# An S5 layer and prompt heads, placed differently against a paged attention

## The chip, the cores and the metric

The kernel runs on one core of a Trainium2 chip. The metric is the device time of one execution in microseconds, given as the median of several runs. Engines are called by the profile's names: PE is TensorE (matmuls and transposes), DVE is VectorE, ACT is ScalarE, POOL is GpSimd, and SP is SyncE, which issues most of the DMA transfers, in program order, from one queue of instructions.

## What is computed

One step of a two-layer decoder, for a prompt of 512 tokens and eight samples of four tokens each (544 columns in all, in most matmuls two halves of 272). Everything is float32. Layer 0 has the even mixer, which the change touches; layer 1, the memory attentions and the MLPs follow.

```python
def even_mixer(hn, pos, h0_re, h0_im, attend, p):
    proj = hn @ p['w_in']
    c_q, c_kv, k_r, u = proj[..., :o1], proj[..., o1:o2], proj[..., o2:o3], proj[..., o3:]
    cq = rms_norm(c_q, p['cq_norm'])
    qf = rms_norm((cq @ p['w_uq']).reshape(b, L, MLA_HEADS, MLA_QK), p['q_gain'])
    q = jnp.concatenate([qf[..., :MLA_NOPE], rope(qf[..., MLA_NOPE:], pos)], axis=-1)
    ckv = rms_norm(c_kv, p['ckv_norm'])
    kr = rope(k_r[:, :, None, :], pos)[:, :, 0]
    o_att = attend(q, ckv, kr).reshape(b, L, MLA_HEADS * MLA_V)
    o_s5, hr, hi = s5_ssm(u, h0_re, h0_im, p)
    return jnp.concatenate([o_att, o_s5], axis=-1) @ p['w_out'], ckv, kr, hr, hi
```

`attend` is causal attention over the prompt (8 heads) for the prompt rows. For the samples it is attention over 16 pages of 128 cached latent rows each (8 samples, so 128 pages), plus the four new tokens. `s5_ssm` is a complex diagonal recurrence over 32 groups of 16 channels with 64 states each, followed by a GELU and a gate: `z * sigmoid(z @ w_glu + b_glu)`.

## The kernel before

`even_mixer` first transposes x into h (the residual, [128, 8, 544], kept in SBUF to the end), then projects: u (S5's input), cq, ckv, q, and kv. Every weight comes through `load_w`: an SP load (wraw), a split into a high and a low part on ACT (wH) and DVE (wL), and three matmuls per product. The tile framework's scheduler orders the engines' instructions by its own estimates, except on SP in `decode_attention`, where `manual_schedule` keeps the order of the code.

`s5_layer` is called between the u and the cq projection, and the scheduler mixes its work into all the projections that follow. It has four tiles (4 x 128 channels). Of each tile, `s5_tables_of` builds tables on DVE and POOL (s5tmp, s5W, s5T, s5w), `s5_gather` fetches U by 16 small DMAs, and `s5_tile` runs the recurrence: matmuls s5X, products on DVE and POOL (s5g), scans on DVE, Hp, and 160 matmuls s5Y. A GELU (zt, z) and a split (zH, zL) follow. `s5_out` is the gate (glu, 96 matmuls) after kv.

`decode_attention` runs over 64 steps: 8 samples with 8 pairs of pages. In a step each page has its latents transposed (ct), split (cH, cL), and multiplied (24 kp matmuls for a pair, kp has two PSUM buffers); ACT squares kp (sq), DVE reduces the square (L1156) and adds the scores (L1155), and POOL raises the sums to the power -0.5 (L1161, once in two steps). `load_pages(b + 1)` first reads 16 page numbers (`page_numbers`, one register load each on SP), then issues 16 rope loads (krn) and 16 latent loads (cnat). It is called at page 4 of sample b, after `batch_end(b - 1)`, which does the softmax and the values of the sample before. At page 14 of a sample one prompt head is emitted (`prompt_head`: pqk transposes, four rounds of scores S, maximum, exponential Pm, transposes pPT, and then po), with three at sample 5, from q_tok, k_tok and v_tok in SBUF. At the end `beside` projects the memory (mkv, 192 matmuls), whose weights are loaded during sample 7, and then comes the output projection (ps_wo, 384 matmuls).

Of the kernel before, what the change touches and what calls it, by code (L numbers as in the profile page):

```python
# [105 lines left out]
class K:  # L106
    def __init__(self, tc, a, o, ctx):
# [11 lines left out]
        self.h = self.cp.tile([128, KT, NT], F32, name="h")  # L119
# [198 lines left out]
    def even_mixer(self, gs, beside):  # L318
# [11 lines left out]
        self.uT = utile("uT", F32)  # L330
        rs.enter_context(self.gemm_pools("left"))
        IN = main("even_in")
        s5s, cqs = ExitStack(), ExitStack()
        SP = s5s.enter_context(self.pool("s5main", side="left"))
# [5 lines left out]
        L = xp.tile([128, KT, NT], F32R, name="xgL")  # L340
        xts = self.load_x([CQ.tile([128, 6, NT], F32, tag=f"cq{x}", bufs=1, name=f"x{x}") for x in "HL"])
# [10 lines left out]
        self.s5_params(SP)  # L352
# [44 lines left out]
        self.gemm(w, KT, 0, 6, (H, L), ev, "cq")  # L397

# [32 lines left out]
        Q = qs.enter_context(self.pool("qkv", side="right"))  # L431
# [33 lines left out]
        for ch in range(2):  # L465
            wq = self.load_wk(a["w_mla_uq"][0], 6, 384 * ch, 384, f"uq{ch}")
            hs = slice(4 * ch, 4 * ch + 4)
            for t in (4, 0, 1, 2, 3):
# [23 lines left out]
                nc.vector.tensor_tensor(out=q[:, :, NOPE:], in0=q[:, :, NOPE:], in1=tmp[:rows], op=ALU.add)  # L492
        self.sample_heads(qTs, q_s, self.qgain)
# [36 lines left out]
        s5t.close()  # L530
        cqs.close()
        pg = self.page_numbers(0)
        self.s5_out()
        self.oatt = utile("oatt", F32)
        s5s.close()
        rs.close()
        gs.close()
        with ExitStack() as ds:
            dp = ds.enter_context(self.pool("dec1", side="left"))
            dp2 = ds.enter_context(self.pool("dec2", bufs=2, side="left"))  # L540
            ap = qs.enter_context(self.pool("patt", bufs=2, side="right"))
# [17 lines left out]
    def prompt_head(self, h, p, q_tok, k_tok, v_tok):  # L559
# [3 lines left out]
        for dst, src, gain in ((qT, q_tok, self.qgain), (kT, k_tok, 1.0)):  # L563
            ps = self.att_ps("pqk")
            for t in range(4):
                self.transpose(ps[:QK, t * 128:(t + 1) * 128], src[:, t, h, :])
# [22 lines left out]
        for j in range(4):  # L589
            c = b if j in (0, 3) else 64 - b  # L590
            nc.tensor.matmul(po[c:c + 64, j * 128:], v_tok[:, j, h, :], PT[:, j, j * 128:], start=(j < 2), stop=(j > 1),
                             skip_group_check=True, tile_position=(0, c))
# [197 lines left out]
    def s5_tables_of(self, ft, p, E):  # L790
# [6 lines left out]
        R = {}  # L797
        tmp = lambda: p.tile([128, 512], F32, tag="s2k", bufs=4, name="s5tmp")
# [3 lines left out]
        for i, (x, y, op) in enumerate((("bbr", "bbi", B), ("bbi", "bbr", A))):  # L802
            t1, t2 = [tmp()[:, :256].rearrange("p (q j c) -> p q j c", q=4, j=4) for _ in range(2)]
# [1191 lines left out]
```

## Time and profile before

| | us |
|---|---|
| median of the runs (3) | 1976.15 |
| lowest and highest | 1973.0, 1979.17 |
| profiled execution, its own time | 1978.92 |
| its span | 1977.2 |
| first kp of sample 0 | 254.5 |
| first kp of sample 4 | 411.2 |
| start of the last kp | 573.2 |
| first matmul of the output projection | 600.7 |

The span is what the profile covers. A window is a stretch of the span, with the busy time of each engine in it. The busy time of PE counts each matmul from its start to its modelled end, and matmuls overlap, so that the price of a matmul in a row of equal ones is the distance of two starts. The chain that ended last follows the work back from the last instruction, at each step to what released it.

### The profile page before, as it was taken

What the parts mean: (1) busy time and instruction counts of PE and PEld (TensorE: products, weight loads), DVE (VectorE), ACT (ScalarE), POOL (GpSimd) and SP (SyncE); (2) the same over time, 40 slices, a digit from 0 to 9 for tenths busy, and PEclk for the clock granted to TensorE, in tenths of its full rate; (3) what the DMA queues carried; (4) which work ended last, traced back from release to release, by engine and by line L of the source; (5) the groups of instructions that cost most, each with busy time, mean ns of one, the idle gap of its engine ahead of it and who ended that gap; (6) DMA issues with size and microseconds to landing.
All of it is one profiled execution on the core that took longest, in us unless ns stands there. A gap on an engine that the chain in (4) does not pass through costs nothing.

```text
span 1977.2 us, 39933 instructions
## 1 busy us (share of the span) xinstructions
PE 1911.8 (97%) x16089; PEld 1803.5 (91%) x16089; DVE 1165.2 (59%) x2264; ACT 804.5 (41%) x1546; POOL 471.4 (24%) x375
## 2 busy tenths in 40 slices
PE   8888899999999999999999999999999999999998
PEld 7876688889889979999999999999999799999998
DVE  7776566666765557433333568898865663434344
ACT  4455454455564444322222334444443432313131
POOL 4555246655552205000000110111132130000000
PEclk9988999999999999999999999999999999999999
DMA  6221221222334453322322332323325233223222
GB/s 151 72 56 36 69 69 49 67 74 52 100 107 99 141 174 95 95 86 87 95 86 86 91 100 83 104 78 97 91 70 168 91 105 87 86 87 95 86 86 78
DMA packets 317162, 179.42 MB, mean 91 GB/s; under 512 B 52241, under 2 KB 305266, under 8 KB 316978
## 3 DMA queue, kind: packets, MB, share of 16 engines
q1 hardware_dynamic: 289154, 164.47, 28.8%
q10 hardware_dynamic: 26224, 8.06, 1.7%
q0 software_dynamic: 1600, 4.34, 0.8%
q8 instruction: 127, 2.08, 0.4%
q14 instruction: 57, 0.47, 0.1%
HBM read 165.90 MB, written 9.82 MB: 89 GB/s over the span
## 4 chain that ended last, share of the span: by engine, by line
PE 88%; DVE 4%; ACT 2%; issue 2%; SPq 2%; DMA 1%; POOL 1%; ACTq 0%; DVEq 0%; POOLq 0%
PE ps_dn L191 19%; PE ps_up L191 19%; PE kp L1151 9%; PE ps_wo L191 5%; PE ps_hq L191 3%; PE ps_hi L191 3%; PE ps_hf L191 3%; PE ps_hg L191 2%; PE ps_mq L191 2%; PE ps_wmo L191 2%; PE mkv L191 2%; PE ps_u L191 1%; SPq L1026 1%; PE ct L290 1%; PE q L191 1%
## 5 line engine op out<-in xcount | busy, mean ns | idle before, releaser
L191 PE MATMUL ps_dn<-hidH,wH_dn 128*128 128x272 f32 x1024 | 211.4, 287 | 0.0
L191 PE MATMUL ps_dn<-hidH,wL_dn 128*128 128x272 f32 x1024 | 211.2, 288 | 0.0
L191 PE MATMUL ps_up<-actH_f,wH_up 128*128 128x272 f32 x1024 | 211.2, 287 | 0.0
L191 PE MATMUL ps_dn<-hidL,wH_dn 128*128 128x272 f32 x1024 | 210.7, 287 | 0.0
L191 PE MATMUL ps_up<-actH_f,wL_up 128*128 128x272 f32 x1024 | 210.5, 288 | 0.0
L191 PE MATMUL ps_up<-actL_f,wH_up 128*128 128x272 f32 x1024 | 210.4, 287 | 0.0
L1161 POOL TENSOR_TENSOR ss<-ss,nhalf 128x32 f32<-128x32 f32 x32 | 173.7, 5429 | 96.1 <-DVE ss L1159 92.9
L1266 DVE TENSOR_TENSOR h<-ps_dn,h 128x544 f32<-128x544 f32 x64 | 46.4, 725 | 207.1 <-PE ps_dn L191 207.1
L191 PEld LDWEIGHTS ps_dn<-hidL,wH_dn 128*128 128x128 f32 x1024 | 160.2, 188 | 0.0
L191 PEld LDWEIGHTS ps_up<-actL_f,wH_up 128*128 128x128 f32 x1024 | 160.0, 188 | 0.0
L191 PEld LDWEIGHTS ps_dn<-hidH,wL_dn 128*128 128x128 f32 x1024 | 159.6, 189 | 0.1
L191 PEld LDWEIGHTS ps_dn<-hidH,wH_dn 128*128 128x128 f32 x1024 | 159.5, 188 | 0.0
L191 PEld LDWEIGHTS ps_up<-actH_f,wL_up 128*128 128x128 f32 x1024 | 159.4, 188 | 0.0
L191 PEld LDWEIGHTS ps_up<-actH_f,wH_up 128*128 128x128 f32 x1024 | 159.4, 188 | 0.0
L166 ACT ACTIVATE wH_dn<-wraw_dn 128x1024 fp32r<-128x1024 f32 x64 | 68.1, 1064 | 216.5 <-PE ps_dn L191 154.8
L166 ACT ACTIVATE wH_up<-wraw_up 128x1024 fp32r<-128x1024 f32 x64 | 68.1, 1063 | 195.0 <-PE ps_up L191 99.1
L167 DVE TENSOR_TENSOR wL_up<-wraw_up,wH_up 128x1024 fp32r<-128x1024 f32 x64 | 83.5, 1305 | 107.8 <-ACT wH_up L166 105.7
L167 DVE TENSOR_TENSOR wL_dn<-wraw_dn,wH_dn 128x1024 fp32r<-128x1024 f32 x64 | 78.3, 1224 | 67.5 <-ACT wH_dn L166 65.3
L1154 ACT ACTIVATE sq<-kp 128x512 f32<-128x512 f32 x128 | 76.5, 597 | 95.6 <-PE kp L1151 56.1
L254 POOL TENSOR_TENSOR acc_x<-acc_x,sq 128x544 f32<-128x544 f32 x7 | 10.8, 1540 | 349.6 <-issue 327.2
L1156 DVE TENSOR_REDUCE ss<-sq 128x8 f32<-128x512 f32 x128 | 86.8, 678 | 0.0
L166 ACT ACTIVATE hidH<-mu 128x544 fp32r<-128x544 f32 x64 | 42.2, 660 | 101.0 <-DVE mu L1577 101.0
(738 smaller groups left out, 5081.8 us busy)
## 6 DMA issues: line engine op xcount, KB each, us to landing
wraw_up<-in_w_mlp_up_dram SPq DMA_DIRECT2D x64, 512.0 KB, 4.1
wraw_dn<-in_w_mlp_down_dram SPq DMA_DIRECT2D x64, 512.0 KB, 3.7
cnat<-in_cache_mla_latent_dram SPq DMA_DIRECT2D x128, 128.0 KB, 2.2
mkc<-in_cache_mem_k_dram SPq DMA_DIRECT2D x16, 512.0 KB, 6.3
wraw_w_mem_k<-in_w_mem_k_dram SPq DMA_DIRECT2D x8, 512.0 KB, 4.7
wraw_w_mem_v<-in_w_mem_v_dram SPq DMA_DIRECT2D x8, 512.0 KB, 3.7
wraw_wo<-in_w_out_even_dram SPq DMA_DIRECT2D x8, 512.0 KB, 4.0
wraw_mq<-in_w_mem_q_dram SPq DMA_DIRECT2D x8, 512.0 KB, 3.6
```

The source lines that it names most:

```text
L166: i = nc.scalar.activation(H, x, AF.Copy)
L167: sub.tensor_tensor(out=L, in0=x, in1=H.bitcast(F32), op=ALU.subtract)
L191: nc.tensor.matmul(out, x, sl(y), start=first and n == 0, stop=last and n == 2)
L254: nc.gpsimd.tensor_tensor(out=acc, in0=acc, in1=sq, op=ALU.add)
L290: self.nc.tensor.transpose(out, in_, self.ident[:p, :p])
L1026: load = lambda x, t, src: nc.sync.dma_start(x, src[bass.ds(pg[t], 1), 0].rearrange("o t c -> (o t) c"))
L1151: mm = nc.tensor.matmul(ps[:, hf, :272], x[:, t % 2, kt], wb[hf][y][:, kt], start=(kt == 0 and n == 0), stop=(kt == 1 and n == 2))
L1154: nc.scalar.activation(sq, ps[:, :, :256], AF.Square)
L1156: V.tensor_reduce(out=ss[:, t, :], in_=sq.rearrange("p f (h d) -> p (f h) d", h=4), op=A, axis=AX.X)
L1161: G.tensor_tensor(out=sf, in0=sf, in1=self.nhalf, op=ALU.pow)
L1266: self.nc.vector.tensor_tensor(out=halves(self.h[:, i, :]), in0=ps, in1=halves(self.h[:, i, :]), op=ALU.add)
```

## The change

S5 and the gate are taken out of the prologue and become a generator, `mixer_steps`, that `decode_attention` draws from after the page scores of each step. `s5_layer` yields twelve times per tile and `s5_out` five times, each half a step; then comes the load of head 0 (one step) and the eight heads at four steps each, where `load(h + 1)` is issued ahead of head h. For this

- the residual h is stored to DRAM (hd) after the transposes, its SBUF tile is freed, and it is loaded again, in eight pieces, ahead of the output projection;
- q, k and v of the prompt are stored to DRAM (qd, kd, vd: twelve stores) as they are made, their SBUF tiles are freed, and each head loads its three parts into a pool of two buffers;
- S5's temporaries are 256 wide instead of 512 (five buffers), U, w, g and Hp get two buffers, and all PSUM of S5 and the gate is the attention's `at` (two buffers), which the heads use too;
- `s5_params` runs after the cq projection.

The core of the diff:

```diff
@@ even_mixer
+        self.h = hs.enter_context(self.pool("hx", side="right")).tile([128, KT, NT], F32, name="hx")
+        self.hd = self.ctx.enter_context(self.pool("hd", space=bass.MemoryType.DRAM)).tile([128, KT, NT], F32, name="hd")
...
-        self.s5_params(SP)
+        nc.sync.dma_start(self.hd, self.h)
+        hs.close()
...
-        s5t = ExitStack()
-        self.s5_layer(*(s5t.enter_context(self.pool(n, side="left")) for n in ("s5E", "s5tile")))
...
         self.gemm(w, KT, 0, 6, (H, L), ev, "cq")
+        self.s5_params(SP)
...
+                if t < 4:
+                    nc.sync.dma_start(qd[:, :, t, :], q)
...
+            if t < 4:
+                nc.sync.dma_start(kd[:, :, t, :], k_tok[:, t])
+                nc.sync.dma_start(vd[:, :, t, :], v_tok[:, t])
...
-        self.s5_out()
...
-            self.decode_attention(dp, dp2, pg, qTs, kTs, lambda h: self.prompt_head(h, ap, q_tok, k_tok, v_tok), qs,
-                                  beside)
+            self.decode_attention(dp, dp2, pg, qTs, kTs, self.mixer_steps(utile, qs, qd, kd, vd), qs, beside)
...
+    def mixer_steps(self, utile, qs, qd, kd, vd):
+        nc = self.nc
+        with self.pool("s5E", side="right") as pe, self.pool("s5tile", side="right") as p:
+            for _ in self.s5_layer(pe, p):
+                yield 0.5
+        with self.pool("s5glu", bufs=2, side="right") as self.wp:
+            for _ in self.s5_out(self.wp):
+                yield 0.5
+        self.oatt = utile("oatt", F32)
+        ap = qs.enter_context(self.pool("patt", bufs=2, side="right"))
+        def load(h):
+            ts = [ap.tile([128, 4, x.shape[3]], F32, name=n) for n, x in (("q_tok", qd), ("k_tok", kd), ("v_tok", vd))]
+            for t, x in zip(ts, (qd, kd, vd)):
+                nc.sync.dma_start(t, x[:, h])
+            return ts
+        ts = load(0)
+        yield 1
+        for h in range(HEADS):
+            nx = load(h + 1) if h + 1 < HEADS else None
+            self.prompt_head(h, ap, *ts)
+            ts = nx
+            yield 4
@@ s5_tables_of, s5_tile
-        tmp = lambda: p.tile([128, 512], F32, tag="s2k", bufs=4, name="s5tmp")
+        tmp = lambda: p.tile([128, 256], F32, tag="s1k", bufs=5, name="s5tmp")
...
-        ps = self.psA("s5T")
+        ps = self.att_ps("s5T")
@@ decode_attention
-                if t == NPG - 2:
-                    for h in range(b, b + 1 if b < 5 else HEADS if b == 5 else b):
-                        head(h)
+                while due <= n - AHEAD:
+                    due += next(more, len(steps))
@@ before the output projection
+                self.h = es.enter_context(self.pool("h", side="left")).tile([128, KT, NT], F32, name="h")
+                for k in range(KT):
+                    nc.sync.dma_start(self.h[:, k, :], self.hd[:, k, :])
```

How the order changes, at three places. The first is PE where sample 4 takes over from sample 3: krT and krS belong to the keys of sample 4. Before:

```order
1633 L1151 MATMUL kp<-wk11H,cL 128x272
1634 L290 MATMUL krT<-ident,krn_3209 128x128 x4
1635 L1151 MATMUL kp<-wk10H,cH 128x272
...
1654 L1151 MATMUL kp<-wk11H,cH 128x272
1655 L1115 MATMUL krS<-qr,krT 128x128 x4
1656 L1151 MATMUL kp<-wk10L,cH 128x272
```

And now, where rows 1537 to 1632 are the 96 matmuls of the gate:

```order
1536 L980 MATMUL s5Y<-s5U,s5T 32x136 x4
1537 L190 MATMUL glu_5070<-zH_2980,wH_glu_5066 128x272
...
1632 L190 MATMUL glu_5268<-zH_5055,wL_glu_5264 128x272
1633 L289 MATMUL s5f<-ident,s5finp 16x128
...
1638 L289 MATMUL krT<-ident,krn_2039 128x128 x3
1639 L1157 MATMUL krS<-qr,krT 128x128 x4
1640 L289 MATMUL ct<-ident,cnat_2040 128x128 x4
```

The keys of sample 4 stood between kp matmuls of sample 3; now they stand behind the gate, and no kp stands between the last S5 matmul and them.

The second place is PE in a prompt head. Before (head 7, its third and fourth round of scores):

```order
2449 L1151 MATMUL kp<-wk11H,cL 128x272
2450 L290 MATMUL pPT<-ident,Pm 128x128 x3
2451 L572 MATMUL S<-kT,qT 128x512
2452 L574 LDWEIGHTS identb
2453 L574 MATMUL S<-causalb,identb 128x128
2454 L1151 MATMUL kp<-wk10H,cH 128x272
```

And now (head 1, ahead of the first kp of sample 5):

```order
1883 L605 MATMUL S<-causalb,identb 128x128
1884 L289 MATMUL pPT<-ident,Pm 128x128 x3
1885 L603 MATMUL S<-kT,qT 128x512
1886 L605 LDWEIGHTS identb
1887 L605 MATMUL S<-causalb,identb 128x128
1888 L289 MATMUL krT<-ident,krn_2034 128x128 x3
1889 L289 MATMUL pPT<-ident,Pm 128x128 x4
1890 L289 MATMUL krT<-ident,krn_2034 128x128
1891 L622 MATMUL po<-PT,v_tok 64x512
```

The rounds of a head had 12 or 24 kp matmuls between them; of this head and of heads 3, 5 and 7 they follow one another.

The third place is SP ahead of the page numbers (TENSOR_LOAD pt) of sample 5, with what each instruction waits for. Before:

```order
568 L1026 DMA cnat_3210<-in_cache_mla_latent_dram 128x256 [waits DMAHW4_49,PE_49]
569 L1026 ISA
570 L1026 DMA cnat_3210<-in_cache_mla_latent_dram 128x256 [waits DMAHW5_49,PE_49]
571 L1000 TENSOR_LOAD pt
572 L1000 ISA x2
```

And now, where the wait on PE in row 604 is for the output matmuls of head 0:

```order
598 L1068 DMA cnat_2040<-in_cache_mla_latent_dram 128x256 [waits DMAHW2_49]
599 L572 DMA q_tok<-qd 128x384 [waits DMAHW3_49]
600 L572 DMA k_tok<-kd 128x384 [waits DMAHW4_49]
601 L572 DMA v_tok<-vd 128x256 [waits DMAHW5_49]
...
604 L572 DMA v_tok<-vd 128x256 [waits DMAHW0_49,PE_49]
605 L572 DMA q_tok<-qd 128x384 [waits DMAHW3_49,DMAHW1_49,PE_49]
606 L572 DMA k_tok<-kd 128x384 [waits DMAHW4_49,DMAHW2_49,PE_49]
607 L572 DMA v_tok<-vd 128x256 [waits DMAHW5_49,PE_49]
608 L1042 TENSOR_LOAD pt
609 L1042 ISA x2
```

The page numbers stood directly behind the latents of the sample before; now nine loads for three heads stand between. In the same way the four gate weights, which wait for PE, POOL and DVE, stand ahead of the page numbers of sample 4, and loads for heads ahead of those of samples 6 and 7.

## Rows read from the trace of the kernel before

**Rows 1.** The page: busy time by engine, and the chain's shares by engine.

```profile
PE 1911.8 (97%) x16089; PEld 1803.5 (91%) x16089; DVE 1165.2 (59%) x2264; ACT 804.5 (41%) x1546; POOL 471.4 (24%) x375
...
PE 88%; DVE 4%; ACT 2%; issue 2%; SPq 2%; DMA 1%; POOL 1%; ACTq 0%; DVEq 0%; POOLq 0%
```

**Rows 2.** Windows: stretch, us, busy PE, PEld, DVE, ACT, POOL, TensorE clock, DMA share, GB/s.

```profile
0.00:254.00 254.00, 212.91 (x1940) 186.10 (x1941) 176.02 (x415) 128.46 (x348) 117.78 (x171) 0.93 0.30 78
254.00:411.00 157.00, 154.28 (x1232) 138.65 (x1230) 103.56 (x276) 80.08 (x163) 90.05 (x46) 1.00 0.24 62
411.00:573.00 162.00, 160.31 (x1304) 144.74 (x1303) 114.38 (x298) 89.19 (x178) 92.57 (x32) 1.00 0.27 75
573.00:601.00 28.00, 25.48 (x233) 22.36 (x233) 17.19 (x28) 14.63 (x22) 12.37 (x5) 0.94 0.56 169
601.00:1977.00 1376.00, 1358.87 (x11390) 1311.62 (x11388) 754.02 (x1249) 492.19 (x838) 158.64 (x122) 1.00 0.33 97
```

**Rows 3.** Timeline of TensorE (start, us): kp starts sample 0, sample 4, ends sample 7.

```profile
254.50 0.52 PE L1151 MATMUL kp<-wk00H,cH 128*128 128x272 f32 x2
...
411.21 0.37 PE L1151 MATMUL kp<-wk00H,cH 128*128 128x272 f32 x1
...
573.21 0.29 PE L1151 MATMUL kp<-wk11H,cL 128*128 128x272 f32 x1
```

**Rows 4.** Chain that ended last (start, us, what): S5, a transpose group, output matmuls, projection.

```profile
91.03 4.36 PE s5Y L943 x128
...
281.47 0.44 PE ct L290 x4
281.90 1.22 PE po L591 x6
...
600.74 47.98 PE ps_wo L191 x384
```

**Rows 5.** Waits of TensorE, 0 to 254 us: total us, times, longest.

```profile
PE s5Y L943 <- DVE s5Hp L914: 4.3, 5, 1.9
...
PE q L191 <- ACT q_tok L481: 2.7, 2, 2.6
```

**Rows 6.** Windows: a stretch of the prologue, columns as in rows 2.

```profile
135.00:140.00 5.00, 3.20 (x14) 2.65 (x15) 5.00 (x10) 4.39 (x12) 2.22 (x3) 0.50 0.46 111
```

**Rows 7.** Timeline of SyncE's issues (start, us): page loads of three samples.

```profile
240.28 8.28 SPq L1026 DMA_DIRECT2D cnat<-in_cache_mla_latent_dram  x14
258.25 8.82 SPq L1026 DMA_DIRECT2D krn<-in_cache_mla_krope_dram  x16
...
408.69 8.40 SPq L1026 DMA_DIRECT2D krn<-in_cache_mla_krope_dram  x16
431.34 9.85 SPq L1026 DMA_DIRECT2D cnat<-in_cache_mla_latent_dram  x16
```

**Rows 8.** The page's DMA issues: count, KB each, median us to landing.

```profile
cnat<-in_cache_mla_latent_dram SPq DMA_DIRECT2D x128, 128.0 KB, 2.2
```

**Rows 9.** Lines on VectorE, 254 to 411 us: busy, mean ns, idle before.

```profile
L167 DVE TENSOR_TENSOR cL<-ct,cH 128x512 fp32r<-128x512 f32 x32 | 21.9, 684 | 1.2 <-ACT cH L166 1.0
...
L577 DVE TENSOR_REDUCE st<-S 128x1 f32<-128x128 f32 (+3 forms) x16 | 7.7, 484 | 1.3 <-PE S L574 1.2
...
L595 DVE TENSOR_TENSOR oatt<-po,oatt 64x384 f32<-64x384 f32 x4 | 2.2, 556 | 0.5 <-ACT oatt L594 0.4
```

**Rows 10.** Lines on GpSimd in the same stretch.

```profile
L1161 POOL TENSOR_TENSOR ss<-ss,nhalf 128x32 f32<-128x32 f32 x15 | 81.4, 5429 | 38.5 <-DVE ss L1159 37.5 <-DVE S L1155 1.0
```

**Rows 11.** Windows, 50 to 245 us, tile s5tmp (PE, PEld, DVE, ACT, POOL); s5g (no ACT).

```profile
50.00:245.00 195.00, 2.97 (x36) 1.21 (x36) 36.96 (x72) 14.47 (x36) 41.57 (x52) 0.92 0.21 56
...
50.00:245.00 195.00, 11.59 (x256) 8.00 (x256) 30.90 (x48) 14.78 (x24) 0.92 0.21 56
```

**Rows 12.** Timeline of SyncE's issues: the memory weights.

```profile
537.03 20.44 SPq L179 DMA_DIRECT2D wraw_w_mem_k<-in_w_mem_k_dram  x4
561.21 17.87 SPq L179 DMA_DIRECT2D wraw_w_mem_v<-in_w_mem_v_dram  x4
```

More of the change, by code (lines that the diff above doesn't have):

```diff
@@ L430, in even_mixer @@
         kTs = PB.tile([QK, HEADS, NSAMP], F32, name="kTs")
-        Q = qs.enter_context(self.pool("qkv", side="right"))
+        Qs = ExitStack()
+        Q = Qs.enter_context(self.pool("qkv", side="right"))
+        qd, kd, vd = (self.ctx.enter_context(self.pool(n, space=bass.MemoryType.DRAM))
+                      .tile([128, HEADS, 4, d], F32, name=n) for n, d in (("qd", QK), ("kd", QK), ("vd", VD)))
         q_tok = Q.tile([128, 4, HEADS, QK], F32, name="q_tok")
@@ L802, in s5_tables_of @@
         for i, (x, y, op) in enumerate((("bbr", "bbi", B), ("bbi", "bbr", A))):
[L803 removed]
+            t1, t2 = [tmp().rearrange("p (q j c) -> p q j c", q=4, j=4) for _ in range(2)]
             G.tensor_tensor(out=t1, in0=b4(x), in1=a4("Br", 16), op=M)
@@ L869, in s5_gather @@
         NC = NT // 4
-        U = p.tile([128, 4, NC], F32, name="s5U")
+        U = p.tile([128, 4, NC], F32, bufs=2, name="s5U")
         for j in range(4):
@@ L884, in s5_tile @@
         W1, W2, T, w = R["W1"], self.W2, R["T"], R["w"]
-        tmp = lambda n=512: p.tile([128, 512], F32, tag="s2k", bufs=4, name="s5tmp")[:, :n].rearrange("p (q k) -> p q k", k=128)
-        g = p.tile([128, 2, 4, 128], F32, name="s5g")
+        tmp = lambda: p.tile([128, 256], F32, tag="s1k", bufs=5, name="s5tmp").rearrange("p (q k) -> p q k", k=128)
+        g = p.tile([128, 2, 4, 128], F32, bufs=2, name="s5g")
         xs = p.tile([128, 2, 4, NB], F32, name="s5xs")
-        Hp = p.tile([128, 2, 4, NC + 1], F32, name="s5Hp")
+        Hp = p.tile([128, 2, 4, NC + 1], F32, bufs=2, name="s5Hp")
         G.memset(Hp[:, :, :, NB:NB + 1], 0.0)
@@ L971, in s5_layer, with s5_out @@
             self.zL.append(zL)
-    def s5_out(self):
+            yield
+    def s5_out(self, p):
         nc, a, o = self.nc, self.a, self.o
         z2, S = self.z2, self.s5
-        bg = S["bg"]
-        def ev(i, ps):
-            th = self.tp.tile([128, NT], F32, tag="sq", name="glu")
-            nc.scalar.activation(halves(th), ps, AF.Tanh, scale=0.5, bias=bg[:, i:i + 1])
+        for i in range(4):
+            wH, wL = self.load_w(a["s5_w_glu"][0], 0, 4, 128 * i, 128, f"glu{i}")
+            ps = [self.att_ps(f"glu{x}")[:, :HALF] for x in range(2)]
+            for k in range(4):
+                self.mm3([(ps[x], lambda y, x=x: y[:, x * HALF:(x + 1) * HALF]) for x in range(2)],
+                         (wH[:, k, :], wL[:, k, :]), (self.zH[k], self.zL[k]), k == 0, k == 3)
+            th = p.tile([128, NT], F32, name="glu", bufs=1)
+            for x in range(2):
+                nc.scalar.activation(th[:, x * HALF:(x + 1) * HALF], ps[x], AF.Tanh, scale=0.5, bias=S["bg"][:, i:i + 1])
@@ L982, in ev @@
             nc.vector.scalar_tensor_tensor(out=z2[:, i, :], in0=th, scalar=1.0, in1=z2[:, i, :],
                                            op0=ALU.add, op1=ALU.mult)
[L984 to L995 removed]
+            yield
@@ new lines, in s5_out @@
+        fo = p.tile([128, 2, 128], F32, name="s5fo", bufs=1)
+        fp = p.tile([16, 2, 128], F32, name="s5fp", bufs=1)
+        for i, n in enumerate(("s5r", "s5i")):
+            ps = self.att_ps("s5f")
+            self.transpose(ps[:16, 128:256], S["finp"][:, i])
+            self.transpose(ps[:, :128], S["fins"][:, i].rearrange("p b q -> p (b q)"))
+            self.copy(fp[:, i], ps[:16, 128:256])
+            self.copy(fo[:, i], ps[:, :128])
+            nc.gpsimd.dma_start(o[n + "_p"].rearrange("e b (p g) n -> (e b p) (g n)", g=2), fp[:, i])
+            nc.gpsimd.dma_start(o[n + "_s"].rearrange("e b (p g) n -> (e b p) (g n)", g=2), fo[:, i])
@@ L1001, in page_numbers, with decode_attention @@
                 for t in range(NPG)]
-    def decode_attention(self, p, p2, pg, qTs, kTs, head, qs, beside):
+    def decode_attention(self, p, p2, pg, qTs, kTs, more, qs, beside):
         nc, a = self.nc, self.a
```

80 lines of the change are left out of this document (36 added, 44 removed).

## The prediction

> **What bounds the kernel now.** I read the page first: TensorE is busy 97% of the span and carries 88% of the chain that ended last [rows 1]. A share over the whole span hides stages, so next comes the table by stage [rows 2]. From 601 us on (output projection, both memory attentions, both MLPs, odd layer) TensorE is busy 1358.87 of 1376 us and the change leaves that code alone, so everything is decided before 600.74 us, where the output projection starts [rows 4]. There the table shows two different stages. In the prologue (0 to 254 us) TensorE is busy 212.91 us at a granted clock of 0.93, and VectorE 176.02. In the paged attention (254 to 573 us) TensorE is busy 154.28 of 157 and 160.31 of 162 us, at clock 1.00, with VectorE at about two thirds. So the prologue has TensorE time to win and the attention has next to none: whatever is moved from one to the other pays its TensorE price in full, and wins only what TensorE now loses around it.
>
> The borders come from the timeline of TensorE [rows 3]: first key-projection matmul (kp) of sample 0 at 254.50, of sample 4 at 411.21, last one at 573.21. Half the attention, 32 steps and four prompt heads, thus takes 156.7 us; from sample 4 to the output projection it is 189.5 us. Prices: 272 columns cost 47.98/384 = 0.125 us, a 128-column transpose 0.11 (0.44 for four), a head's output matmuls 1.22 [rows 4]. A head is 18 transposes (2.0), the output matmuls (1.2) and score matmuls with bias, which have the same columns (1.3 to 2): 4.5 to 5.3 us, I take 5.3. 128 s5Y matmuls cost 4.36 us [rows 4], all 640 make 21.8, and 196 smaller ones at 0.06 to 0.11 us make 12 to 21: S5 is about 36 us of TensorE. Its gate (glu) is 96 matmuls of 0.125: 12 us.
>
> **The change part by part.**
> 1. *Work that only moves.* The prologue loses S5 and glu: 36 + 12 = 48. The first half of the attention gains S5 and loses four heads: 36 - 21 = +15. The second half gains glu and four heads: 12 + 21 = +33. The sum is zero; TensorE does the same work. So the forecast is a sum of idle time won and lost.
>
> 2. *Idle won in the prologue: -26.* Of the 254 us, 41 are idle and the clock takes 7% of the rest [rows 2]; S5 has part in both. Waits on S5 by name are small: 4.3 us for s5Hp, and ten or so with the smaller ones [rows 5]. Behind them stand the pieces at half clock, such as 135 to 140 us, which began after TensorE had idled [rows 6], and a VectorE that was full there. What stays: loading the first inputs (about 7 us), ScalarE's scaling of q (the wait on q_tok [rows 5]), the handover to the attention. I take 26, between 12 (named waits alone) and 44 (all but start and handover). The first kp would then stand at 254.5 - 48 - 26 = 180 us. The new DRAM copies cost little: q, k and v are twelve stores behind which a few gathers and page loads queue on SyncE, the residual store stands ahead of two weight loads; 0 to 4 us, inside the bounds. The reload of the residual lies under the 48 us of the output projection.
>
> 3. *Idle made in the S5 half: +24.* TensorE has 156.7 + 15 = 172 us to do there. VectorE had 103.56 us [rows 2], of which the heads' five lines (7.7 to 2.2, together 22.5 [rows 9]) leave and S5 comes: 36.96 and 30.90 for the two tile groups [rows 11] and 9 for the activation, 77 us: 158 in all. GpSimd had 90.05 and gets the 41.57 and 14.78 of [rows 11]: nearly 150. Three engines, each at 80 to 90% of 172, working in order on two chains that pass between all of them: a GpSimd power takes 5.43 us [rows 10], and a VectorE step of S5 that waits for a product queued behind it holds up the square-sum and mask steps of the page scores that stand behind it on VectorE, and then kp, which has two buffers. In the prologue the same mix kept TensorE idle 16% of the time; 14% of 172 is 24. Bounds: 3 (the attention's present idle) and 50 (one power's wait in two for 20 hand-overs between VectorE and GpSimd, each 5.43).
>
> 4. *SyncE behind TensorE: +43.* Before, pages are requested long ahead: sample 5's rope pages from 408.69, the latents from 431.34, for a start 40 us after the first [rows 7]. After, SyncE, whose order is fixed by hand, meets waits on TensorE ahead of those requests. The gate's first weights wait for the buffers of the last S5 tile, the third and fourth for VectorE's split of the first, and only then come sample 4's page numbers. From sample 5 on, the load of a head's v waits for the output matmuls of the head two before, and the page numbers of the next sample stand behind it. What a release costs until the next sample's first kp: three issues 0.5, sixteen page numbers 9.7 (248.56 to 258.25 [rows 7]), sixteen rope issues 8.8 [rows 7], a latent issue 0.5, landing 2.2 [rows 8], transpose and its two casts 1.7 [rows 4, 9], 0.5 of hops: 24 us. In TensorE's order the releases stand as follows. Sample 4: release at the end of S5, first weights 4 us, so 27 us with 13.5 of glu and small work under it: 13 idle. Sample 5: head 0's output half a step before its start, so 24 with 2 us of kp and head 1's chain of 7 under it: 15. Sample 6: three steps of 4.2 and head 3 under it: 5. Sample 7: 1.6 steps and head 5: 10. Sum 43. The heads' serial chains (score, maximum, exponential, transpose, no kp between) hide in these gaps; without them they would cost 2 to 4 us each. Bounds: 10 (page numbers come in a third of the time when SyncE has nothing else) and 60.
>
> 5. *Tail: +12.* Before, the memory weights load in 20.44 and 17.87 us under sample 7 [rows 12], and 48 of their 192 matmuls stand between kp. After, the first weight loads wait for buffers until head 7's query and key transposes, in step 62 of 64, and the splits stand behind head 7's copies on ScalarE. Eight loads at 4.8 us are 38 us from there; about 12 lie under the last steps and head 7, and 22 us of matmuls run along. From the last kp to the output projection I get 45 instead of 27.5, of which head 7's 5 is counted above: +12, between 0 and 20.
>
> A rule that speaks against term 4: the Trainium skill, "DMA: Bandwidth & Descriptors", section "Issuing engines are not separate DMA queues", says that the sequencer's time to initiate a transfer is usually small beside the transfer. [rows 7] show the opposite for these pages: 8.8 us of issuing for sixteen transfers of which one lands in about 2 us. By the rule the holds would cost about a landing each and the forecast is rival B below.
>
> **Sum.** -26 + 24 + 43 + 12 = +53 against the profiled execution, 1978.9 us: 2032. That execution was 2.8 us above the median of the runs shown, 1976.15, so the forecast is 2029.
>
> **Rivals.**
> A, faster: TensorE stays the bound throughout. It decides if a S5 tile's chain fits into its eight steps with the head's time freed (43 us of TensorE per tile) and pages are asked for 24 us before a sample ends. Then terms 3 to 5 shrink to 3 + 0 + 0 and -26 stays: 1953. For it: VectorE's and GpSimd's 150 to 158 fit into 172. Against it: SyncE's order, which is fixed, and no row that shows TensorE releasing SyncE early. 6%.
> B, the holds cost little: gaps of 2 us instead of 24, the rest as forecast: 2029 - 43 + 8 = 1994. For it: glu and heads stand in these places and fill them. Against: [rows 7]. 12%.
> C, slower still: S5's hand-overs each meet a power, 50 instead of 24, gaps 60: 2029 + 26 + 17 = 2072. For it: GpSimd near 150 us of work, in order. Against: S5's table work needs no result of the pages and can run ahead by two buffers. 20%.
> D, the change does not do what it says (S5 still in the prologue): TensorE's order has no S5 matmul ahead of the first kp. 1%.
> The forecast, and what lies around it: 61%.
>
> **How the numbers follow.** About 0.3%, 6 us, is what a measurement can tell from no change. Case A and a twentieth of B are faster or the same; B otherwise ends slower, as do C and the forecast, save for a few per cent in which the prologue gives 44 and the S5 half takes 3. Faster 0.08, same 0.04, slower 0.88. For eight in ten the range goes from B's 1994 to a little above C, 2076; I leave A out.
>
> **What the profile after would show.** The first kp near 180 us (172 to 195); the S5 half near 196 us with TensorE busy under 90% and its waits on s5Hp, s5g and S; gaps of 10 to 15 us ahead of samples 4, 5 and 7 that end in cnat, krn or krs, with SyncE idle before page numbers; 40 us or more from the last kp to the output projection, with waits on w_mem's splits. Wrong would be: gaps that are absent although SyncE stands where it does (then a buffer is released earlier than I read), an S5 half under 180 us, or a prologue that ends after 200 us, which would mean that its idle time never came from S5.

## The result, and the profile after

The changed kernel takes 2056.15 us (median) where the kernel before, run beside it, takes 1976.37: a ratio of 1.0404, with a 95% interval of 1.0384 to 1.0425. It is 4% slower. One of the four executions of the changed kernel was slow, 6861.66 us, and is not in the ratio. The forecast was 2029, in a range of 1994 to 2076. The profiled execution of after has a span of 2054.4 us against 1977.2, that is +77.2, and the rest of this section says where they are.

The page of after, busy time by engine and the chain's shares, answers to [rows 1]: TensorE has the same 16089 matmuls but is busy for 37 us more, and SyncE's queue (SPq) and DMA take 6% of the chain instead of 3%.

```profile
PE 1949.0 (95%) x16089; PEld 1821.8 (89%) x16089; DVE 1166.0 (57%) x2280; ACT 808.8 (39%) x1550; POOL 467.5 (23%) x383
...
PE 85%; DVE 4%; ACT 3%; DMA 3%; SPq 3%; issue 2%; POOL 1%; ACTq 0%; DVEq 0%; POOLq 0%
```

The same work at more busy time means that some of it ran at a lower clock. The borders of the stages come from TensorE's timeline of after (start, us, instruction), as in [rows 3]: first kp of sample 0, of sample 4, last kp, and the output projection.

```profile
199.87 0.52 PE L1193 MATMUL kp<-wk00H,cH 128*128 128x272 f32 x2
...
401.81 0.59 PE L1193 MATMUL kp<-wk00H,cH 128*128 128x272 f32 x1
...
615.22 0.29 PE L1193 MATMUL kp<-wk11H,cL 128*128 128x272 f32 x1
...
672.73 1.27 PE L190 MATMUL ps_wo<-mixsH,wH_wo 128*128 128x272 f32 x4 [2.82 <-ACT mixsH L168]
```

Windows of after by stage (stretch, its length, busy PE, PEld, DVE, ACT, POOL with counts, granted TensorE clock, DMA share, GB/s). The second begins with the first kp and ends with S5's last s5Y; the third ends with the last kp.

```profile
0.00:200.00 200.00, 162.44 (x1048) 145.02 (x1049) 103.60 (x281) 83.85 (x235) 64.66 (x89) 0.90 0.49 129
200.00:370.50 170.50, 164.45 (x1841) 146.64 (x1841) 143.14 (x354) 95.51 (x203) 137.67 (x132) 1.00 0.15 39
370.50:615.50 245.00, 213.91 (x1505) 178.59 (x1493) 135.07 (x355) 109.61 (x227) 97.26 (x37) 0.89 0.28 72
615.50:672.70 57.20, 43.43 (x319) 35.34 (x318) 29.48 (x53) 27.03 (x48) 10.97 (x7) 0.81 0.37 106
672.70:2054.00 1381.30, 1364.75 (x11390) 1316.19 (x11390) 754.72 (x1240) 492.86 (x838) 156.95 (x119) 0.99 0.33 99
```

Against the borders of before (254.5, 411.2 and 600.7) the prologue is 54.6 us shorter, the S5 half 13.9 longer (170.6 instead of 156.7), everything from there to the projection 112.7 longer (302.2 instead of 189.5), and the rest 5.2. The work that moved is 48, 15 and 33 by the prediction's prices. So idle time and slow work changed by -7 in the prologue, -1 in the S5 half, and **+80 behind it**. That last stage is cut up here, from S5's end to the last kp:

```profile
370.50:401.80 31.30, 20.09 (x131) 17.65 (x119) 11.27 (x26) 11.24 (x22) 9.92 (x7) 0.83 0.44 79
401.80:439.80 38.00, 38.00 (x290) 33.36 (x290) 22.91 (x66) 17.85 (x36) 15.75 (x4) 0.96 0.21 63
439.80:465.35 25.55, 16.09 (x75) 10.38 (x73) 9.62 (x26) 8.69 (x20) 7.98 (x7) 0.67 0.28 68
465.35:492.70 27.35, 27.35 (x215) 22.69 (x216) 17.93 (x48) 13.04 (x29) 8.07 (x3) 1.00 0.22 63
492.70:519.00 26.30, 22.65 (x140) 18.24 (x137) 15.06 (x39) 11.32 (x25) 15.45 (x8) 0.81 0.31 78
519.00:551.70 32.70, 32.70 (x263) 28.45 (x261) 21.52 (x57) 16.03 (x34) 11.88 (x4) 1.00 0.15 45
551.70:576.85 25.15, 18.39 (x98) 13.65 (x96) 11.61 (x30) 9.35 (x21) 11.23 (x3) 0.73 0.29 74
576.85:615.50 38.65, 38.65 (x310) 34.17 (x307) 25.17 (x68) 22.08 (x46) 16.98 (x4) 1.00 0.33 100
```

Four stretches with gaps, 25 to 31 us each and one ahead of each of the samples 4 to 7, alternate with stretches in which TensorE is busy throughout. They are without any page score for their last 31, 24, 15 and 20 us. In the four together TensorE idles 31 us, and what it does, it does at a mean clock of 0.67 to 0.83. SyncE's timeline of after (start, us, issues) shows what stands ahead of samples 4, 5 and 7: the gate's weights ahead of the first, and ahead of the others the load of a head's v, then sixteen page numbers (about 9.6 us without a row) and the pages. Ahead of sample 6 it is as ahead of 5 and 7.

```profile
328.93 46.28 SPq L178 DMA_DIRECT2D wraw_glu<-in_s_w_glu_dram  x4
384.45 8.92 SPq L1068 DMA_DIRECT2D krn<-in_cache_mla_krope_dram  x16
...
439.61 0.32 SPq L572 DMA_DIRECT2D v_tok<-vd  x1
449.55 8.09 SPq L1068 DMA_DIRECT2D krn<-in_cache_mla_krope_dram  x16
457.82 9.26 SPq L1068 DMA_DIRECT2D cnat<-in_cache_mla_latent_dram  x16
...
551.56 0.32 SPq L572 DMA_DIRECT2D v_tok<-vd  x1
561.18 8.09 SPq L1068 DMA_DIRECT2D krn<-in_cache_mla_krope_dram  x16
```

From the issue of v_tok to the next sample's first kp are 25.7 us (465.35 - 439.61), and 25.3 ahead of sample 7. Who held SyncE is in its waits, 370 to 620 us (total us, times, longest): a head's output matmuls three times, S5's last tile, and for the memory weights a head's transposes.

```profile
SPq L572 <- PE po L622: 79.2, 3, 28.3
SPq L178 <- PE s5Y L980: 40.8, 1, 40.8
SPq L178 <- PE pqk L289: 14.5, 1, 14.5
```

All this is as the prediction had it. But what TensorE waited for there is not only pages. Its waits, 370 to 615.5 us:

```profile
PE krT L289 <- DMA krn<-in_cache_mla_krope_dram: 13.0, 9, 2.7
PE pPT L289 <- DVE Pm L612: 11.0, 8, 2.6
```

The second row is a prompt head waiting for its own softmax. TensorE's timeline in the gap ahead of sample 5 shows head 1 done there in one piece:

```profile
442.85 0.49 PE L603 MATMUL S<-kT,qT 96*128 96x128 f32 x2 [0.78 <-ACT kT L598]
...
444.88 0.30 PE L289 MATMUL pPT<-ident,Pm 128*128 128x128 f32 x1 [1.48 <-DVE Pm L612]
...
452.07 0.87 PE L289 MATMUL pPT<-ident,Pm 128*128 128x128 f32 x3 [2.56 <-DVE Pm L612]
...
459.54 2.40 PE L622 MATMUL po<-PT,v_tok 128*64 128x512 f32 x8
```

A head for which the prediction counted 5.3 us of TensorE's time takes 19 alone, from its first scores to the end of its output matmuls (442.85 to 461.94). So is the gap long because the pages come late, or are the heads the cost, and the gap merely where they stand? The experiments ask that.

### The profile page after: what moved, and what is told of

Same layout as the page of the kernel before. It is cut to its first block, busy times and chain, and to the rows that moved or that the text cites. A ratio compares the mean times of both kernels' runs of the same rounds, so it can differ in the third digit from the quotient of the medians.

```text
span 2054.4 us, 39993 instructions
## 1 busy us (share of the span) xinstructions
PE 1949.0 (95%) x16089; PEld 1821.8 (89%) x16089; DVE 1166.0 (57%) x2280; ACT 808.8 (39%) x1550; POOL 467.5 (23%) x383
## 4 chain that ended last, share of the span: by engine, by line
PE 85%; DVE 4%; ACT 3%; DMA 3%; SPq 3%; issue 2%; POOL 1%; ACTq 0%; DVEq 0%; POOLq 0%
PE ps_dn L190 19%; PE ps_up L190 19%; PE kp L1193 7%; PE ps_wo L190 5%; PE ps_hq L190 3%; PE ps_hi L190 3%; PE ps_hf L190 2%; PE ps_wmo L190 2%; PE ps_hg L190 2%; PE ps_mq L190 2%; PE ps_cq L190 2%; SPq L1068 1%; PE ct L289 1%; PE s5Y L980 1%; PE q L190 1%
## 5 line engine op out<-in xcount | busy, mean ns | idle before, releaser
L166 DVE TENSOR_TENSOR wL_dn<-wraw_dn,wH_dn 128x1024 fp32r<-128x1024 f32 x64 | 78.3, 1224 | 67.5 <-ACT wH_dn L165 65.3
```

Of the source, the lines that this page charges most:

```text
L166: sub.tensor_tensor(out=L, in0=x, in1=H.bitcast(F32), op=ALU.subtract)
```

## Experiments

Each ratio is to the kernel before, run on the same chip beside it. **Holds** is the prediction's step 4: SyncE waits for TensorE ahead of the page numbers, and pages come late. **Chains** is the rival (**crowding**, in the last two expectations): eight heads start only behind S5 and gate, a head among page scores takes 6 to 7 steps at about one round of scores per step, eight don't fit into the 31 steps that are left, and those left over stand alone, each for its whole serial chain.

### Taking the holds away

With more buffers for a head's q, k and v its loads wait for an older head, so that ahead of sample 5 (three buffers), or of all of the samples 5 to 7 (four), none holds page numbers up for long. The edit of the two (bufs is 3 in the first, 4 in the second):

```diff
-ts = [ap.tile([128, 4, x.shape[3]], F32, name=n) for n, x in ...]
+ts = [ap.tile([128, 4, x.shape[3]], F32, name=n, bufs=4) for n, x in ...]
```

> One number is changed: the q, k and v tiles of a head get three buffers instead of two. The third head's load then waits for nothing ahead of sample 5's page numbers; the loads ahead of samples 6 and 7 still wait, for the head before last but two. Theory 'holds' (SyncE standing behind TensorE makes the gaps): the gap ahead of sample 5 (63.5 us from the first kp of sample 4 to that of sample 5, against 39 before) closes to about 43, those ahead of 6 and 7 stay, the time is about 2056 - 20 = 2036. Rival 'chains' (eight heads, each a chain of four rounds over three engines, do not fit in 32 steps at one round per step, and the gaps only gave them a place): the gap closes too, but the last head moves behind the last kp and the tail (57.5 us from last kp to output projection) grows by 12 or more, so that the time stays at 2048 or above.

> The same with four buffers: no load of a head waits for a head that is not long done, and in the built order no long run of head instructions without a kp stands ahead of samples 5, 6 and 7 any more. Theory 'holds': all three gaps close (63.5, 53.6 and 57.9 us from first kp to first kp become about 43 each), 2056 - 45 = about 2011. Rival 'chains': the gaps close, but two heads move behind the last kp, whose chains of about 13 us each have nothing beside them: tail 57.5 + 26, time about 2035.

Three buffers: 2059.89 us, 1.0413 (1.0382 to 1.0445). Sample 4 lasts 40.9 us instead of 63.5, sample 5 50.1, but sample 6 65.3, and the tail (last kp to projection) 79.5 instead of 57.5. Four buffers: 2050.08, 1.0364 (1.0334 to 1.0394). All three gaps are gone, samples 4 to 6 take 42.3, 39.7 and 41.0 us, and the tail takes 108.1. Windows of the kernel with four buffers, sample 4 to the last kp, and the tail:

```profile
400.20:561.20 161.00, 160.88 (x1279) 142.98 (x1279) 107.97 (x295) 83.64 (x170) 86.21 (x29) 0.99 0.31 86
561.20:669.30 108.10, 72.42 (x416) 50.51 (x414) 43.16 (x88) 41.84 (x83) 11.97 (x9) 0.70 0.22 66
```

The attention itself is now as full as before [rows 2], and the time went behind it. TensorE's waits in that tail begin with the softmax, and its timeline shows one head after another; from the first scores of one to those of the next are 21.9 us:

```profile
PE pPT L289 <- DVE Pm L612: 17.4, 10, 2.5
```

```profile
588.75 0.49 PE L603 MATMUL S<-kT,qT 96*128 96x128 f32 x2 [0.68 <-ACT kT L598]
...
610.64 0.80 PE L603 MATMUL S<-kT,qT 96*128 96x128 f32 x2 [0.68 <-ACT kT L598]
```

The holds make the gaps; but of 80 us their removal gives 8 back, with an uncertainty of about 7. Both results lie nearer to the rival's expectations (2048 or above, and 2035) than to those of the holds (2036 and 2011). Four buffers took 15 us more than the rival said, too: three heads stand behind the last kp and not two.

### The gate later

The gate's weights stand on SyncE ahead of sample 4's page numbers. Here they come 2.5 steps later.

```diff
+        yield 2.5
         with self.pool("s5glu", bufs=2, side="right") as self.wp:
```

> After S5 the mixer waits 2.5 steps before it asks for the gate's weights, so that sample 4's page numbers and pages stand ahead of them on SyncE; the heads start 2.5 steps later. Theory 'holds': the gap ahead of sample 4 goes (31 us from the last S5 matmul to sample 4's first kp, of which 15 are gate and keys), about -14; the heads' gaps stay where they are: 2042. Rival 'chains': the heads begin later by 2.5 steps (10 us) and their last chain moves behind the last kp, so that the tail gives back 10 or more: 2052.

2067.16 us, 1.045 (1.042 to 1.048). The gap ahead of sample 4 goes (sample 3 lasts 50.3 us instead of 78.4) and comes back in sample 4 (94.3 instead of 63.5). The heads begin later, and the tail is 63.7: a loss of 11 us. Neither theory had expected one (2042 and 2052).

### The handover

The splits of wk, which stand ahead of the copies of wkT in the code, were put behind them.

```diff
-            for i in range(2): ... self.split(v(wk[i][hf][0]), v(wk[i][hf][1]), wraw[...])
             qd = pc.tile([128, 4, 2, NSAMP], F32, name="qd")
...
+            for i in range(2): ... self.split(...)
             ps = self.att_ps("snew")
```

> Only the order of the setup of the paged attention is changed: the split of the key weights (wk) is written behind the transposed key weights (wkT) and qabs instead of ahead of them. TensorE waits 6.3 and 2.4 us for wkT between the last kv matmul (177.7) and the first kp (199.9). Theory: this handover of 22 us, over which the gate used to lie, is why the prologue gave 6.6 us of idle time and not 26; with wkT first the first kp comes about 5 us earlier and the time is about 2051. Rival: SyncE, which issues twelve stores and sample 1's pages until 199, sets the first kp; then nothing moves (2056).

2055.89 us, 1.0393 (1.034 to 1.0446). The wait that it was to end, qabs for wkT, is still there (7.0 us): the scheduler kept VectorE's order. So this tells nothing of the idea, only that the place in the code doesn't set it.

### The heads' price in both kernels

Heads and their loads left out, the prompt's part of the attention output set to zero; in the changed kernel, and then in the kernel before.

```diff
-        ts = load(0)
-        yield 1
-        for h in range(HEADS): ...
+        for x in self.oatt:
+            nc.gpsimd.memset(x[:, NSAMP:], 0.0)
+        yield 33
```

```diff
                 if t == NPG - 2:
-                    for h in range(b, b + 1 if b < 5 else HEADS if b == 5 else b):
-                        head(h)
+                    pass
```

> The prompt's heads and their loads are left out (their columns of the attention's output are zeros), everything else is as in the changed kernel. Theory 'chains': the heads are what stretches the second half and the tail; without them the first kp of samples 5 to 7 follow at 35 to 37 us, the memory weights load under sample 7 as before the change, the tail is about 28 us, and the time is 2056 - 100 = about 1955; only the gap ahead of sample 4 stays, which is the gate's. Rival 'holds' in a wide form (it is SyncE's order, and the gate's and memory's weights alone would hold it too): the tail stays near 50, time about 1985.

> The kernel before the change with the prompt's heads left out (their columns of the attention's output are zeros). It tells what eight heads cost where they are spread over 64 steps, beside e5, where leaving them out of the changed kernel gave 101 us. Theory 'chains': before the change a head costs TensorE's own time and no more, 8 x 5.3 = 42 us: about 1936. Rival 'heads are dear everywhere' (their waits on VectorE and ScalarE cost as much before): 1978 - 80 or more, 1898 or below.

The changed kernel without heads: 1954.97 us, 24.9 below the kernel before (0.9888; 0.9805 to 0.9971). So the heads cost 105 us in it, with some 16 of uncertainty from this run. The kernel before without them: 1935.76, 42.8 below (0.9777; 0.9743 to 0.9812), or 5.35 for a head, the price that the prediction used. The heads' matmuls are the same in both. One part of the first expectation missed: the changed kernel's tail without heads is 37.2 us and not 28.

### Shortening the chain

The scores of round i + 1 are written ahead of the transposes of round i, so that a round's softmax has them as cover; first with two buffers as in the change, then with four.

```diff
+        S = scores(0)
         for i in range(4):
...
             nc.scalar.activation(Pm[:, :n], S[:, :n], AF.Exp, bias=st[:, 0:1], accum_out=st[:, 1:2])
+            S = scores(i + 1) if i < 3 else None
```

> In a head the scores of round i + 1 are written ahead of the transposes of round i, so that a round's maximum runs while the round before is still scaled and transposed; buffers and loads stay as in the changed kernel. Theory 'chains': a head that stands alone shrinks from 17 to 22 us to about 13, the gaps ahead of samples 5 to 7 and head 7's part of the tail shrink by 4 to 6 us each, and as head 7 ends earlier the memory's weights do too: 2056 - 25 = about 2030. Theory 'holds': the releases of SyncE move by as little as a third of that: 2048.

> Four buffers and the overlapped rounds together. Theory 'chains': nothing stands ahead of samples 5 to 7 (40 to 42 us from first kp to first kp), and the two heads behind the last kp cost 13 us each instead of 22: 2050 - 20 = about 2030. Theory 'holds' has nothing left to win here: 2050.

Overlapped rounds alone: 2025.4 us, 1.0244 (1.0198 to 1.0289), with every hold in place. Both edits: 2026.98, 1.0252 (1.0206 to 1.0297). A shorter chain gives 31 us, and taking the holds away gives nothing more on top. TensorE's wait for the softmax, from 370 us to the projection, falls to 2.3 us where it was 16.8 (11.0 and 5.8 in the tail):

```profile
PE pPT L289 <- DVE Pm L617: 2.3, 4, 1.1
```

### Heads late in the kernel before

The kernel before, with two heads at the end of each of the samples 3 to 6 in the code.

```diff
-                    for h in range(b, b + 1 if b < 5 else HEADS if b == 5 else b):
+                    for h in (range(2 * b - 6, 2 * b - 4) if 2 < b < 7 else ()):
                         head(h)
```

> The kernel before the change, S5 in the prologue, q, k and v in SBUF, no loads of heads; only the heads are moved: two at a time, at the ends of samples 3, 4, 5 and 6, so eight heads in the last 34 steps. Theory 'chains' in its simple form (eight heads at one round per step need about 40 steps): the last two run behind the last kp or hold samples up, 1978 + 30 or more. Rival 'crowding is harmless' (the heads fit in four steps each as long as nothing else holds them, so what hurts in the changed kernel is that they begin at step 33, behind the gate, and that the memory's weights wait for their buffers): 1978 to 1985.

1983.4 us, 1.0023 (1.0008 to 1.0038). In TensorE's order the heads stand where they stood before, within about a step (0, 5, 14, 22, 30, 38, 46 and 53): the scheduler put them back. So crowding wasn't tried here, and the run decides nothing.

### Heads beside S5

The heads start with S5 at step 0, one every 6.5 steps, with overlapped rounds; S5's pieces are 0.8 of a step, and ScalarE issues the head loads and S5's gathers. To make room S5's tiles and the head's temporaries have one buffer, and a head's output goes to DRAM.

```diff
+        gens = [heads(), s5()]
+        while min(at) < 1000:
+            i = 0 if at[0] <= at[1] else 1
...
-                nc.sync.dma_start(t, x[:, h])
+                nc.scalar.dma_start(t, x[:, h])
...
-        w = R["w"] = p.tile([128, 2, 4, 128], F32, bufs=2, name="s5w")
+        w = R["w"] = p.tile([128, 2, 4, 128], F32, name="s5w")
...
+        nc.scalar.dma_start(self.od[b:b + 64, h // 2], out)
```

> The changed kernel with both S5 and the heads drawn over all 64 steps: the heads' loads start at step 0, one head per 6.5 steps, S5 at 0.8 instead of 0.5 step per piece, the gate 4.1 steps after it; rounds overlapped as in e6; to make room S5's w, g, Hp and the heads' qT, kT and Pm have one buffer, s5tmp four, and a head's output goes to DRAM and comes back ahead of the output projection; the loads of heads and of S5's U are issued by ScalarE. Theory 'chains': with 64 steps for eight chains the gaps and the long tail go, the time is what TensorE has to do, between 1972 and 1990. Rival 'too much beside the pages' (S5's and the heads' work together overload VectorE, ScalarE and the two score buffers): 2000 or more.

2030.82 us, 1.0253 (1.0222 to 1.0283). Windows of this kernel, samples 0 to 5, sample 6, and from there to the projection:

```profile
196.60:474.95 278.35, 264.84 (x2469) 231.83 (x2468) 198.97 (x513) 149.44 (x325) 177.06 (x143) 0.98 0.24 65
474.95:559.50 84.55, 70.80 (x592) 57.93 (x592) 52.38 (x131) 35.11 (x76) 37.28 (x21) 0.84 0.15 42
559.50:649.00 89.50, 77.17 (x622) 68.69 (x620) 51.05 (x118) 46.05 (x85) 33.15 (x16) 0.92 0.45 119
```

Through sample 5 the heads lie beside S5 at a clock of 0.98. But S5 now lasts into sample 6, and its last tile, the gate and head 6 stand there without page scores beside them. The page scores are missing there because of a hold again: the gate's first weights wait on SyncE for S5's last tile, and sample 7's page numbers stand behind them; its first pages are asked for at 543.15 us (SyncE's waits, 380 to 649 us):

```profile
SPq L178 <- PE s5Y L1001: 67.9, 1, 67.9
```

A better place for the heads costs S5 its own, and 25 us are all that is won over the change. The overlapped rounds alone, which this kernel has too, had won 31: the new places gave nothing on top of them, and the 1972 to 1990 expected of them did not come. The time lies where that expectation's rival had put it (2000 or more), but with this hold in it the run does not show that too much work beside the pages is the reason.

### Four heads, with and without holds

Heads 0 to 3 only, the output of the others zero: first eight steps apart in the code, so that no head load holds page numbers up shortly before they are needed (the longest wait of a head load for TensorE is 4.7 us, some 40 us ahead of its sample), then four apart as in the change.

```diff
-        for h in range(HEADS):
+        for x in self.oatt[2:]:
+            nc.gpsimd.memset(x[:, NSAMP:], 0.0)
+        for h in range(4):
...
-            yield 4
+            yield 8
```

> The changed kernel with heads 0 to 3 only, eight steps apart in the code; heads 4 to 7 are left out and their output is zero. In the order built for TensorE the four heads begin at steps 33, 39, 46 and 53 and end by step 59, one round of scores per step, and no head load stands ahead of page numbers on SyncE behind a TensorE wait. Without heads the kernel takes about 1955 us (e5), with eight 2056. Theory 'crowding' (the heads cost more only because eight do not fit behind the gate): four heads, all covered by page scores, cost their TensorE work, 4 x 5.35 = 21, and the change ends near 1978 (1972 to 1987), with gaps ahead of samples 5 to 7 gone (40 to 43 us per sample). Theory 'each head costs 12.6 us behind the gate' (101/8, whatever stands around it): 1955 + 50 = 2005.

> The same four heads at the four steps of the changed kernel (heads 4 to 7 left out, their output zero). Here head 2's and head 3's loads stand ahead of the page numbers of samples 5 and 6 on SyncE, waiting for the output matmuls of heads 0 and 1, as in the changed kernel, while the work is that of e11. Theory 'holds' (term 4 of the prediction): the gaps ahead of samples 5 and 6 cost 15 and 5 us and more, so 20 to 35 us above e11. Theory 'crowding alone': the gaps come, but head 1 is done in one piece inside the first, the attention's work is not more, and the time is within 6 us of e11.

Apart: 1974.6 us, 0.9982 (0.9967 to 0.9998). Held: 1996.11, 1.0079 (1.0058 to 1.0101), 21.5 us more with the same work. Windows of the two, from sample 4's first kp to the projection in the first; the one gap, ahead of sample 5, in the second:

```profile
402.50:594.00 191.50, 188.51 (x1541) 168.77 (x1540) 129.51 (x323) 104.32 (x201) 97.38 (x37) 0.99 0.35 101
```

```profile
443.80:469.60 25.80, 16.30 (x76) 10.61 (x76) 9.85 (x26) 8.92 (x20) 8.19 (x7) 0.67 0.28 74
```

Both theories hold, then, and for different amounts. Four heads fit behind the gate without any loss to be seen: 191.5 us where the kernel before took 189.5. The other four are the loss. In this kernel and in the one with four buffers no hold leaves a gap ahead of samples 5 to 7, and they differ by 76 us for four heads (71.9 above the kernel before, 4.2 below it): 19 a head, and not 5.35. That is a mean of two kinds. With four buffers a fifth head still lies among page scores, as 31 steps at 6 to 7 for a head allow, and the last three stand alone from 562.7 to 629.9 us, 22 each. Behind them it is another 39 us to the projection, with all matmuls of the memory in them, whose weights waited on SyncE for the last head's transposes. Their first issue in that kernel:

```profile
609.99 27.43 SPq L178 DMA_DIRECT2D wraw_w_mem_k<-in_w_mem_k_dram  x4
```

And one hold costs 21 us where the heads would have fitted; with eight, three holds cost 8, since the heads in their gaps would otherwise stand alone in the tail.

So the +79.8 of the medians are: 55 for crowding (76 less the 21 that four heads cost before), 8 for the holds on top, and 17 for the rest, which has the gate's gap, less what the prologue won (71.9 - 76 + 21). By the intervals the first two are uncertain by about 7 each. The two pairs with and without heads give the sum of these two another way: 105 - 43 = 62.

## Why the prediction was right, and where it wasn't

The sign, the holds and the place of the gaps came out, and the time stayed inside the range. The sum did so partly by luck, as the steps show:

**1, work that only moves: right.** The S5 half took 170.5 us; 156.7 + 15 had been 172. A head's 5.3 is 5.35 by the two kernels of before with and without heads.

**2, prologue: -26 forecast, -7 measured.** The 7 lie below the prediction's lower bound of 12. The first kp stands at 199.87 and not at 180, just inside the bound that the prediction gave for "its idle time never came from S5". The last kv matmul went from 229.42 to 177.27, by 52 us, 36 of which are S5: 16 of idle time were won up to there. But the handover gave 10 of them back. Before, the 12 us of the gate stood between the last kv and wkT, and TensorE did not wait for wkT; after, wkT follows kv at once, and TensorE waits (timelines of before and of after, in brackets the wait):

```profile
229.42 0.39 PE L191 MATMUL kv<-wH_ukv,cTL 128*128 128x512 f32 x1
...
244.79 1.03 PE L290 MATMUL wkT<-ident,wukv 128*128 128x128 f32 x8
...
246.53 1.90 PE L1063 MATMUL qabs<-qd,wkT 128*128 128x64 f32 x16
```

```profile
177.51 1.04 PE L289 MATMUL wkT<-ident,wukv 128*128 128x128 f32 x8
...
181.77 1.10 PE L1105 MATMUL qabs<-qd,wkT 128*128 128x64 f32 x8 [2.35 <-ACT wkT L149]
189.16 1.97 PE L1105 MATMUL qabs<-qd,wkT 128*128 128x64 f32 x8 [6.29 <-DVE wkT L147]
```

What failed in this step: it counted the handover among what stays, and not that the gate had been its cover. That is read from the two timelines; the run on the handover could not test it.

**3, S5 half: +24 forecast, -1 measured.** By the prediction's own sign, a half under 180 us, this step was wrong. TensorE is busy 164.45 of 170.5 us there at clock 1.00, though VectorE is busy for 143.14 and GpSimd for 137.67 (window 200 to 370.5 above). The sizes of their work, 158 and 150, were near; the share of idle time taken over from the prologue, 14%, was not. S5's hand-overs between the two engines hardly reached kp (its waits for VectorE's score sums, 200 to 370.5 us):

```profile
PE kp L1193 <- DVE S L1197: 4.1, 7, 1.1
```

The argument against rival C, that the table work can run ahead, fits this; no run tests it.

**4, SyncE behind TensorE: +43 forecast, +55 measured** (from S5's end to the last kp 244.7 us instead of 162.0, less 12 for the gate and 16 for three heads). The chain of causes is in the trace as written, link by link: 25 us from a release to the next kp (24 forecast), gaps ahead of samples 4 to 7, and 21.5 for one hold where it is alone (15 forecast for that sample). In the four windows TensorE idles 11.2, 9.5, 3.7 and 6.8 us where 13, 15, 5 and 10 had been forecast. The rest is busy time of TensorE beyond the prices, in these windows at a clock of 0.67 to 0.83; this step had no term for it. The Trainium skill, "DMA: Bandwidth & Descriptors", section "Issuing engines are not separate DMA queues", says that the time a sequencer takes to initiate a DMA is usually small beside the DMA itself. For one page this trace roughly agrees: sixteen latent issues took 9.26 us (457.82 above), 0.6 each, and one such transfer lands in a median of 2.4 (DMA issues of after, last number):

```profile
cnat<-in_cache_mla_latent_dram SPq DMA_DIRECT2D x128, 128.0 KB, 2.4
```

The prediction read the opposite out of sixteen issues against one landing. What counts here is that all sixteen stand in one queue, behind sixteen page numbers: the time that followed a release was the forecast's kind and not rival B's.

What failed is one sentence of this step: that the heads' chains "hide in these gaps; without them they would cost 2 to 4 us each". Without the gaps the last four heads cost 19 each. The prediction had priced a head at its TensorE work wherever it stands. It had the eight heads at four steps each in the diff, but didn't ask how many steps a head's chain takes among page scores. Before, a head had eight steps of the 64; after, there are 31 steps for eight heads of 6 to 7. Had the forecast been undone by more buffers, as it implies (2029 - 30 or so), it would have been wrong by 50 us.

**5, tail: +12 forecast, +25 measured** (57.5 us instead of 27.5, less the 5 of head 7, which is in step 1; the prediction had 45). SyncE's first memory weights waited for pqk and came at 608.32, as said. Added to it are head 7's chain, whose rounds stand alone from 615.83 to 634.6, and a clock of 0.81.

The errors are +19 in term 2, -25 in term 3, +12 in term 4 and +13 in term 5. With 5 us behind the start of the output projection and 3 by which spans and medians differ, they make the 27 us between forecast and result. That is the luck: the idle time that S5 did not make paid for most of what the prologue and the tail cost more.

## To carry to other kernels

A chain of small dependent steps costs its engine time only while other work stands between its links, so before such work is moved count the steps of cover that each chain needs and those that are left, not the engine time. When a wait is found and its price is known, ask what else stands in its gap: if that work has no other cover, removing the wait moves the loss and doesn't end it. And a block that is taken out of a stage may have been the cover for a handover behind it.

## What the hardware showed

- TensorE's granted clock fell in stretches in which it idled in short pieces: 0.67 in the gap of 439.8 to 465.35, 0.70 in the 108 us tail with four buffers. In the three stretches of after at clock 1.00 behind S5 it was busy throughout. Idle time alone does not settle it: the last 35.0 us ahead of the projection with four held heads (581.8 to 616.8) had 5.1 us of it at clock 1.00. The price can be read from mkv matmuls of equal shape behind the last head: starts 0.21 us apart at the lower level (1.2 GHz; granted clock 0.50 from 641.4 to 647 us), 0.12 at the higher (2.4 GHz; 1.00 from 647.3 to 650), in TensorE's timeline of after:

```profile
641.77 0.41 PE L190 MATMUL mkv<-wL_w_mem_k,memH 128*128 128x256 f32 x1
641.98 0.41 PE L190 MATMUL mkv<-wH_w_mem_k,memH 128*128 128x256 f32 x1
...
649.03 0.28 PE L190 MATMUL mkv<-wH_w_mem_k,memH 128*128 128x256 f32 x1
649.15 0.28 PE L190 MATMUL mkv<-wL_w_mem_k,memH 128*128 128x256 f32 x1
```

- Sixteen page numbers take SyncE about 9.6 us (439.93 to 449.55) also right behind a hold, with nothing issued between; the prediction had left open that they come in a third of that.
- VectorE and GpSimd busy for 84% and 81% of the S5 half left TensorE 6 us idle in 170.5 at clock 1.00, while in the handover, with little other work beside it, it stood through two waits of 2.4 and 6.3 us.
